# The first pair's down projection in each SwiGLU: seven products of Strassen's form, or the plain product by halves of tokens

## The chip, the cores and the metric

The kernel runs on one core of one Trainium2 chip. The metric is the device time of one launch in microseconds; below it is 2633.43 us, the median of three runs (2632.23 to 2636.09). A core has a matrix engine (TensorE, PE in the profile; its weight loads are listed apart as PEld), a vector engine (VectorE, DVE), a scalar engine (ScalarE, ACT), GpSimd (POOL) and a queue that issues the loads (SyncE, SP). Each works through its own queue in order, and they wait for one another by semaphores.

## The reference, cut to what matters

Two groups of tokens (512 and 256) go through two layers with shared weights. Each layer is a half SwiGLU, a mixer, and another half SwiGLU; so there are four SwiGLUs, all of one shape (D_MODEL 1024, D_FF 2816).

```python
def swiglu(h, wg, wu, wd):
    return (jax.nn.silu(h @ wg) * (h @ wu)) @ wd

def even_layer(x, ...):
    x = x + 0.5 * swiglu(rmsnorm(x, f1_n), f1_g, f1_u, f1_d)
    x = x + mixer_ab(rmsnorm(x, mix_n), ...)
    x = x + 0.5 * swiglu(rmsnorm(x, f2_n), f2_g, f2_u, f2_d)
    return x
...
```

The odd layer has another mixer, and a last norm follows. All of it is in float32.

## The kernel before

All 768 tokens are worked on together, features on partitions: x is eight tiles of 128 x 768. Tokens are cut into two halves of 384 (HALVES). Each float32 product is made of three faster matmuls: an operand is split into a rounded high part and the low rest, and `mm3` adds high by high, high by low and low by high into one PSUM bank. For a weight block of 128 x 512, `wsplit` does this with a cast on ScalarE (line 114, tile whi) and a subtraction on VectorE (line 115, wlo), with five tiles of each; for an activation of 128 x 384, `split` does the same (lines 196 and 197).

The 2816 hidden features are 22 blocks of 128, taken as 11 pairs. Within a pair, gate and up are computed by Strassen's method: seven products of half-size blocks in place of eight, where the blocks are halves of the inner dimension, the two feature blocks of the pair, and the two halves of tokens. Sums of weight blocks are made on VectorE (`sums`, line 609, tiles s); sums of products are made in PSUM, with copies of a bank to another (ScalarE) where a partial result is used twice. The products of a pair are called p1 to p7 and read the operands b11, b21, t1, t2, t3, n4, b22. Pairs 0 to 3 are "early": their p1 and p2 are done ahead, in the order of ORDER, so that the second half of the tokens can be normalised meanwhile. The other five follow pair by pair: p6 (t2), p7 (t3), p4 (n4), p5 (t1), p3 (b22), each with a gate and an up product of 12 matmuls. `hidden` turns the finished gate and up of one feature block i and one half of tokens into the tile h[i, half] (VectorE, ScalarE, VectorE, VectorE).

The down projection is done per two pairs, also by Strassen's method. For it, `operands(q)` prepares from the four tiles h of pair q the seven operands b11, t1, b21, t2, t3, b22, n4 (tiles d, each split into high and low; subtractions at line 432). It is a generator: the steps are taken one at a time among the products of pair q + 1, and what is left is done at its end. After pair 1, `down` runs for pair 0 alone; after pairs 3, 5, 7 and 9 it runs for the two pairs before. Pairs 9 and 10 are done plainly at the end by `down_last`, from operands made by `last_operands`. In `down`, each of the seven products splits its weight block (a sum, or a raw block), and for each of four output blocks j sums 3 matmuls for each pair into a bank. Then the bank is copied to another (line 655, ScalarE) or added into x on VectorE (line 661). The product t1 goes into four accumulators acc, which are added into x in two places at the end of the SwiGLU: in the first call this is a copy on ScalarE (line 659), later an addition on VectorE (line 661).

Weights come in raw tiles of 128 x 1024 (512 KB) by a load on SP, in a pool of four (`raw`, line 99). Each pair takes four of them (gate and up of two blocks), each down projection two for each of its pairs. PSUM has two pools of four banks, mm and aux (`psum`).

The order of TensorE's instructions is that of the program. The other engines' instructions are put in order when the kernel is built, by a list scheduler that works with priorities in program order and estimated durations; on the chip that order is fixed. `mm3` also calls `tick`, which lets chains of other work (norms, operands of the next stage) put in their next step when the planner's own clock is due.

Of the kernel before, what the change touches and what calls it, by code (L numbers as in the profile page):

```python
# [14 lines left out]
ALU = mybir.AluOpType  # L15

P = 128
D = 1024
# [5 lines left out]
H = T // 2  # L24
GROUPS = ((0, TA), (TA, T))
HALVES = ((0, H), (H, T))
# [25 lines left out]
class Trunk:  # L52
# [364 lines left out]
    def ffn(self, pre):  # L417
# [7 lines left out]
        acc = []  # L425
        d, dl = {}, {}

        def operands(q):


            h = hs.pop(q)
            sub = lambda o, x, y: nc.vector.tensor_tensor(out=o, in0=x, in1=y, op=ALU.subtract)
            d[q] = {}

            def put(n, src):
                d[q][n] = self.dtile(n), self.dtile(n)
                self.split(*d[q][n], src)

            h11, h12, h21, h22 = h[0, 0], h[0, 1], h[1, 0], h[1, 1]
            yield put("b11", h11)  # L440
            yield sub(h11, h12, h11)
            yield put("t1", h11)
            yield put("b21", h21)
            yield sub(h11, h22, h11)
            if q and q % 2 == 0:
                self.later = operands_2(h, sub, put)
                return
            for _ in operands_2(h, sub, put):
                yield

        def operands_2(h, sub, put):
            h11, h12, h21, h22 = h[0, 0], h[0, 1], h[1, 0], h[1, 1]
            yield put("t2", h11)
            yield sub(h12, h22, h12)
            yield put("t3", h12)
            yield put("b22", h22)
            yield sub(h21, h21, h11)
            yield put("n4", h21)

        def pair(p):  # L460
# [114 lines left out]
            if p:  # L575
                steps = operands(p - 1) if p < NPAIR - 1 else self.last_operands(dl, 0, hs[p - 1], acc)
# [10 lines left out]
        for p in range(NPAIR):  # L587
            for _ in stages[p]:
                pass
            if p == 1:  # L590
                acc += [self.fw.tile([P, H], F32, tag=f"p1{j}", name=f"p1{j}") for j in range(4)]
            if p % 2 and p < NPAIR - 1:
                self.down(pre, range(max(p - 2, 0), p), d, acc)
        kind = self.following[0]
        self.norm_begin(self.following)
        if kind == "f":
# [10 lines left out]
    def sums(self, a11, a12, a21, a22, s, n, name):  # L607

        f = lambda o, x, y, op: self.nc.vector.tensor_tensor(out=o, in0=x, in1=y, op=op)  # L609
        if name == "s1":  # L610
            return s[n, "s1"]
        if name == "s4":
            t = s[n, "s2"]
            f(t, a12, t, ALU.subtract)
            return t
        if name == "s2":
            t = s[n, "s1"] = self.fw.tile([P, 4, P], F32, tag="s", name="s1", bufs=8)
            f(t, a21, a22, ALU.add)
        t = s[n, name] = self.fw.tile([P, 4, P], F32, tag="s", name=name, bufs=8)
        if name == "s3":  # L620
            f(t, a11, a21, ALU.subtract)
        else:
            f(t, s[n, "s1"], a11, ALU.subtract)
        return t

    def dtile(self, name):
        return self.fw.tile([P, H], F32R, tag="e", name=f"d{name}", bufs=NE)

    def down(self, pre, pairs, d, acc):

        nc = self.nc
        a, s, bank = {}, {}, {}
        for p in pairs:
            rows = [self.raw(f"{pre}_w_down", 2 * p + k, 1, 0, D)[:, 0, :] for k in (0, 1)]
            a[p] = [t[:, i * 512 : (i + 1) * 512].rearrange("p (a b) -> p a b", a=4) for i in (0, 1) for t in rows]
        sums = lambda name: {p: self.sums(*a[p], s, p, name) for p in pairs}

        def product(w, b, key, start, out, to=None):  # L640

            st = {p: self.wsplit(w[p], nc.vector) for p in pairs}
            for j in range(4):
                new = lambda k: (self.psum(self.aux, "aux") if k in "YZ" else self.psum())[:, :H]
                if start:
                    bank[key, j] = new(key)
                ps = bank[key, j]
                for p in pairs:
                    self.mm3(
                        ps, (st[p][0][:, j, :], st[p][1][:, j, :]), d[p][b],  # L650
                        start and p == pairs[0], p == pairs[-1], not start,
                    )
                if to:
                    bank[to, j] = new(to)
                    nc.scalar.copy(bank[to, j], ps)
                if out:
                    o = acc[j] if out is acc else self.x[4 * out[0] + j][:, HALVES[out[1]][0] : HALVES[out[1]][1]]
                    if out is acc and pairs[0] == 0:
                        nc.scalar.copy(o, ps)
                    else:  # L660
                        nc.vector.tensor_tensor(out=o, in0=ps, in1=o, op=ALU.add)  # L661

        def more(n):
            for _ in range(n if len(pairs) > 1 else 0):
                next(self.later, None)

        w = {n: {p: a[p][i] for p in pairs} for i, n in enumerate(("a11", "a12", "a21", "a22"))}
        s2 = sums("s2")
        product(sums("s1"), "t1", "Z", True, acc)
        product(w["a11"], "b11", "X", True, None, "Y")  # L670
        more(3)
        product(w["a12"], "b21", "X", False, (0, 0))
        more(1)
        product(s2, "t2", "Y", False, None, "W")
        more(3)
        product(sums("s3"), "t3", "Y", False, (1, 1))
        product(sums("s4"), "b22", "W", False, (0, 1))
        product(w["a22"], "n4", "Y", False, (1, 0))
# [886 lines left out]
```

## Time and profile before

| | |
|---|---|
| Median of three runs | 2633.43 us (2632.23 to 2636.09) |
| The profiled execution | 2634.87 us |
| Its span, first to last instruction | 2633.1 us |
| Granted TensorE clock, mean | 0.99 |
| TensorE busy, instructions | 2561.3 us (97%), 15094 matmuls |
| VectorE busy | 2267.8 us (86%) |
| ScalarE busy | 1365.6 us (52%) |
| DMA | 84 GB/s over the span |

Busy time is the time in which an engine has an instruction at work; instructions of an engine overlap a little in the records, so the mean of one is somewhat longer than the distance to the next. The chain that ended last follows the execution back from its end, at each step to what released it. The four down projections of pair 0 lie at 102.42 to 116.98, 853.45 to 868.01, 1346.82 to 1361.38 and 2201.31 to 2215.87 us of the span.

### The profile page before, as it was taken

How to read it: one execution, taken by the hardware profiler on the slowest of the kernel's cores; microseconds unless marked ns; L12 is line 12 of the kernel's file. 1: busy time of each engine (PE TensorE's matmuls, PEld its weight loads, DVE VectorE, ACT ScalarE, POOL GpSimd, SP SyncE). 2: the span in 40 equal slices, each digit the busy share in tenths (PEclk: the TensorE clock that was granted, in tenths of full speed). 3: DMA queues.
4: the chain of work that ended last, by engine and by line, in shares of the span. 5: the costliest groups of instructions: out<-in, count | busy, mean ns of one | idle time of the engine just before them, and what ended most of it. 6: DMA issues, size and time to landing. Idle time of an engine off the chain costs nothing.

```text
span 2633.1 us, 41175 instructions
## 1 busy us (share of the span) xinstructions
PE 2561.3 (97%) x15094; PEld 2491.3 (95%) x15094; DVE 2267.8 (86%) x4793; ACT 1365.6 (52%) x2851; POOL 88.0 (3%) x172
## 2 busy tenths in 40 slices
PE   7999999998999999999999999999999999999997
PEld 7999999987899999999999999989998989999997
DVE  8998889889779988898999888886777699988886
ACT  7544444555655544454654544454545465454443
POOL 0000000000100000000000000001222100000000
PEclk9999999999999999999999999999999999999998
DMA  5423222421223222222322222232221332222221
GB/s 168 133 78 103 71 81 65 145 87 37 89 77 97 81 81 77 68 75 86 96 81 81 73 73 74 88 111 63 63 63 40 105 104 81 81 71 74 68 87 54
DMA packets 83898, 218.99 MB, mean 83 GB/s; under 512 B 20080, under 2 KB 32880, under 8 KB 83696
## 3 DMA queue, kind: packets, MB, share of 16 engines
q1 hardware_dynamic: 83552, 216.34, 26.5%
q8 instruction: 118, 1.93, 0.3%
q14 instruction: 84, 0.69, 0.1%
q10 hardware_dynamic: 144, 0.03, 0.0%
HBM read 206.90 MB, written 15.07 MB: 84 GB/s over the span
## 4 chain that ended last, share of the span: by engine, by line
PE 86%; DVE 9%; ACT 2%; DMA 2%; issue 1%; SPq 0%; DVEq 0%; ACTq 0%
PE ps_mm L140 54%; PE ps_aux L140 31%; DMA raw<-in_w 1%; DVE wlo L115 1%; PE ps_aux L144 1%; DVE s L609 1%; DVE xl L739 1%; ACT p L911 1%; DVE p L920 0%; DVE p L905 0%; DVE tl L197 0%; ACT whi L114 0%; ACT xh L738 0%; DVE ol L197 0%; DVE x L706 0%
## 5 line engine op out<-in xcount | busy, mean ns | idle before, releaser
L114 ACT CAST whi<-s 128x512 fp32r<-128x512 f32 x496 | 304.9, 621 | 390.6 <-DVE s L609 133.1
L114 ACT CAST whi<-raw 128x512 fp32r<-128x512 f32 x512 | 311.0, 619 | 257.8 <-PE ps_mm L140 116.8
L115 DVE TENSOR_TENSOR wlo<-s,whi 128x512 fp32r<-128x512 f32 x496 | 337.0, 685 | 61.1 <-ACT whi L114 60.8
L115 DVE TENSOR_TENSOR wlo<-raw,whi 128x512 fp32r<-128x512 f32 x494 | 337.5, 691 | 28.3 <-ACT whi L114 24.1
L140 PE MATMUL ps_aux<-dt,whi 128*128 128x384 f32 x864 | 219.3, 334 | 2.1 <-ACT whi L114 2.1
L140 PE MATMUL ps_mm<-db,whi 128*128 128x384 f32 x864 | 219.2, 334 | 0.0
L140 PEld LDWEIGHTS ps_aux<-dt,whi 128*128 128x128 f32 x864 | 156.0, 188 | 2.4 <-ACT whi L114 2.4
L140 PEld LDWEIGHTS ps_mm<-db,whi 128*128 128x128 f32 x864 | 156.1, 188 | 0.0
L140 PE MATMUL ps_mm<-xh,whi 128*128 128x512 f32 (+1 forms) x416 | 147.4, 354 | 3.8 <-ACT xh L738 3.8
L140 PE MATMUL ps_aux<-dt,wlo 128*128 128x384 f32 x432 | 144.4, 334 | 0.3 <-DVE wlo L115 0.3
L140 PE MATMUL ps_mm<-db,wlo 128*128 128x384 f32 x432 | 144.4, 334 | 0.0
L140 PE MATMUL ps_mm<-xl,whi 128*128 128x512 f32 (+1 forms) x416 | 142.3, 342 | 1.1 <-DVE xl L739 1.1
L140 PE MATMUL ps_mm<-xh,wlo 128*128 128x512 f32 (+1 forms) x416 | 142.1, 341 | 0.0
L609 DVE TENSOR_TENSOR s<-raw 128x512 f32<-128x512 f32 x124 | 85.0, 686 | 23.0 <-DMA raw<-in_w 22.9
L499 DVE TENSOR_TENSOR u<-ps_aux,u 128x384 f32<-128x384 f32 x176 | 97.0, 551 | 2.8 <-PE ps_aux L140 2.6
L609 DVE TENSOR_TENSOR s<-raw,raw 128x512 f32<-128x512 f32 x124 | 83.7, 686 | 18.2 <-DMA raw<-in_w 18.0
L140 PE MATMUL ps_aux<-dh,whi 128*128 128x384 f32 x384 | 97.6, 335 | 0.6 <-DVE x L706 0.6
L911 ACT ACTIVATE p<-p,st 128x256 f32<-128x256 f32 (+3 forms) x144 | 68.9, 480 | 55.0 <-DVE st L909 54.9
L494 ACT COPY u<-ps_mm 128x384 f32<-128x384 f32 x176 | 83.5, 474 | 24.2 <-PE ps_mm L140 24.0
L661 DVE TENSOR_TENSOR x<-ps_aux,x 128x384 f32<-128x384 f32 x160 | 86.0, 552 | 9.3 <-PE ps_aux L140 9.2
L140 PEld LDWEIGHTS ps_mm<-xh,whi 128*128 128x128 f32 x416 | 79.9, 192 | 14.1 <-ACT xh L738 4.9
L140 PE MATMUL ps_mm<-oh,whi 128*128 128x384 f32 x256 | 88.1, 344 | 4.6 <-DVE x L888 4.0
(486 smaller groups left out, 8058.2 us busy)
## 6 DMA issues: line engine op xcount, KB each, us to landing
raw<-in_w SPq DMA_DIRECT2D x350, 512.0 KB, 3.7
xdm<-x SPq DMA_DIRECT2D x16, 384.0 KB, 2.3
x<-in_x SPq DMA_DIRECT2D x16, 192.0 KB, 5.5
x<-xdm SPq DMA_DIRECT2D x8, 384.0 KB, 3.4
xold<-xdm SPq DMA_DIRECT2D x8, 384.0 KB, 3.0
out_y<-y SPq DMA_DIRECT2D x8, 384.0 KB, 2.4
tab<-skew SPq DMA_DIRECT2D x8, 256.0 KB, 4.8
raw<-in_w SPq DMA_DIRECT2D x8, 256.0 KB, 2.6
```

The costliest lines, as they stand in the source:

```text
L114: nc.scalar.copy(hi, src)
L115: (eng or nc.gpsimd).tensor_tensor(out=lo, in0=src, in1=hi.bitcast(F32), op=ALU.subtract)
L140: self.nc.tensor.matmul(out, lhsT=lhsT, rhs=rhs, start=start, stop=stop, **kw)
L144: self.nc.tensor.transpose(out, src, self.ident)
L494: nc.scalar.copy(e[n, out], bank[key, n])
L499: nc.vector.tensor_tensor(out=t, in0=bank[key, n], in1=t, op=ALU.add)
L609: f = lambda o, x, y, op: self.nc.vector.tensor_tensor(out=o, in0=x, in1=y, op=op)
L661: nc.vector.tensor_tensor(out=o, in0=ps, in1=o, op=ALU.add)
L739: nc.vector.scalar_tensor_tensor(out=lo, in0=src, scalar=gain, in1=hi.bitcast(F32), op0=ALU.mult, op1=ALU.subtract)
L911: nc.scalar.activation(outs[i], outs[i], AF.Exp, bias=nm[:, i : i + 1], accum_out=sm[:, i : i + 1])
```

## The change

In each SwiGLU, the down projection of pair 0 no longer uses Strassen's products. `operands(0)` splits the four tiles h as they are, and a new function `down_first` multiplies them by the raw weight blocks: for two halves of the output columns (i), four output blocks (j) and two halves of tokens, six matmuls go into one bank (two feature blocks, three matmuls each), and the bank is added into x. The banks of the first half of tokens are from the pool mm, those of the second from aux. Nothing of pair 0 goes into acc, so the first call of `down`, now that of pairs 1 and 2, fills acc by the copy on ScalarE. `more` always takes its steps, as `down` is no longer called for a single pair.

```diff
             def put(n, src):
-                d[q][n] = self.dtile(n), self.dtile(n)
+                name = n if isinstance(n, str) else "h"
+                d[q][n] = self.dtile(name), self.dtile(name)
                 self.split(*d[q][n], src)
 
             h11, h12, h21, h22 = h[0, 0], h[0, 1], h[1, 0], h[1, 1]
+            if q == 0:
+                for i, half in h:
+                    yield put((i, half), h[i, half])
+                return
...
             if p % 2 and p < NPAIR - 1:
-                self.down(pre, range(max(p - 2, 0), p), d, acc)
+                if p == 1:
+                    self.down_first(pre, d[0])
+                else:
+                    self.down(pre, range(p - 2, p), d, acc)
...
+    def down_first(self, pre, d):
+
+        rows = [self.raw(f"{pre}_w_down", k, 1, 0, D)[:, 0, :] for k in (0, 1)]
+        for i in (0, 1):
+            st = [self.wsplit(t[:, i * 512 : (i + 1) * 512].rearrange("p (a b) -> p a b", a=4), self.nc.vector) for t in rows]
+            for j in range(4):
+                for half, (c0, c1) in enumerate(HALVES):
+                    ps = (self.psum(self.aux, "aux") if half else self.psum())[:, :H]
+                    for k in (0, 1):
+                        self.mm3(ps, (st[k][0][:, j, :], st[k][1][:, j, :]), d[k, half], k == 0, k == 1)
+                    x = self.x[4 * i + j][:, c0:c1]
+                    self.nc.vector.tensor_tensor(out=x, in0=ps, in1=x, op=ALU.add)
...
-                    if out is acc and pairs[0] == 0:
+                    if out is acc and pairs[0] == 1:
                         nc.scalar.copy(o, ps)
...
         def more(n):
-            for _ in range(n if len(pairs) > 1 else 0):
+            for _ in range(n):
                 next(self.later, None)
```

## The prediction

> **What bounds the kernel now.** I read the page first: the shares of the engines and the chain that ended last.
>
> ```profile
> span 2633.1 us, 41175 instructions
> ...
> PE 2561.3 (97%) x15094; PEld 2491.3 (95%) x15094; DVE 2267.8 (86%) x4793; ACT 1365.6 (52%) x2851; POOL 88.0 (3%) x172
> ...
> PE 86%; DVE 9%; ACT 2%; DMA 2%; issue 1%; SPq 0%; DVEq 0%; ACTq 0%
> ```
>
> TensorE is busy for 97% of the span and is 86% of the chain; VectorE comes second, 86% busy and 9% of the chain. So a matmul that is added is paid in full unless it falls into a wait, and VectorE work that is removed is worth only the waits of TensorE that it ends. The question is how long those waits are around the four down projections of pair 0. I found these stages in the timeline by the tiles that the matmuls read and asked for the busy time in each: the stage itself, the stretch of pair 1 ahead of it, the stretch of pair 2 behind it. The first number of a row is the stretch, then come the busy times of the engines; PEclk is the granted clock.
>
> ```profile
> core 0: us, PE busy (x) PEld busy (x) DVE busy (x) ACT busy (x) POOL busy (x), PEclk, DMA share, GB/s
> 102.42:116.98 14.56, 14.56 (x85) 14.56 (x85) 14.41 (x28) 9.57 (x21) 0.00 (x0) 1.00 0.34 110
> ...
> sum 58.24, PE 58.24 PEld 58.24 DVE 56.34 ACT 38.32 POOL 0.00; mean PE 14.56 PEld 14.56 DVE 14.09 ACT 9.58 POOL 0.00
> ```
>
> Inside the stage TensorE never waits: 14.56 us in each SwiGLU, all busy, at full clock. But VectorE is full too (56.34 of 58.24 us). The stretches of pair 1 (five products, 120 matmuls) and of pair 2 (the same), summed over the four SwiGLUs:
>
> ```profile
> sum 84.04, PE 83.78 PEld 83.14 DVE 81.98 ACT 48.85 POOL 0.00; mean PE 20.94 PEld 20.79 DVE 20.50 ACT 12.21 POOL 0.00
> ...
> sum 93.70, PE 87.72 PEld 84.32 DVE 90.77 ACT 47.61 POOL 0.00; mean PE 21.93 PEld 21.08 DVE 22.69 ACT 11.90 POOL 0.00
> ```
>
> From the chain, a run of matmuls without any wait gives the price of one:
>
> ```profile
> 191.17 16.64 PE ps_mm L140 x96
> ```
>
> 16.64 / 96 = 0.1733 us, so 120 matmuls need 20.80 us and four such stretches 83.20. Pair 1 loses 84.04 - 83.20 = 0.84 us in all, pair 2 loses 93.70 - 83.20 = 10.50. Nearly all of that sits in its first step, the two t2 products of p6 (24 matmuls, 4.16 us each time):
>
> ```profile
> 116.98:123.32 6.34, 4.73 (x26) 4.10 (x26) 6.30 (x12) 2.09 (x5) 0.00 (x0) 1.00 0.34 91
> 868.01:874.32 6.31, 4.70 (x25) 4.06 (x25) 6.26 (x12) 2.07 (x5) 0.00 (x0) 1.00 0.28 80
> 1361.38:1366.74 5.36, 4.71 (x25) 4.07 (x25) 5.36 (x11) 3.57 (x7) 0.00 (x0) 1.00 0.34 96
> 2215.87:2223.67 7.80, 6.18 (x25) 5.55 (x25) 7.71 (x14) 2.55 (x5) 0.00 (x0) 0.79 0.23 68
> sum 25.81, PE 20.32 PEld 17.78 DVE 25.64 ACT 10.27 POOL 0.00; mean PE 5.08 PEld 4.45 DVE 6.41 ACT 2.57 POOL 0.00
> ```
>
> 25.81 - 16.64 = 9.17 us lost, with VectorE busy throughout (25.64). The timeline of the first SwiGLU shows why:
>
> ```profile
> 110.78 0.33 SPq L99 DMA_DIRECT2D raw<-in_w  x1
> ...
> 111.46 2.12 DVE L661 TENSOR_TENSOR x<-ps_aux,x 128x384 f32<-128x384 f32 x4
> 113.54 2.12 DVE L661 TENSOR_TENSOR x<-ps_mm,x 128x384 f32<-128x384 f32 x4
> 115.62 2.12 DVE L661 TENSOR_TENSOR x<-ps_aux,x 128x384 f32<-128x384 f32 x4
> 117.66 0.68 DVE L609 TENSOR_TENSOR s<-raw 128x512 f32<-128x512 f32 x1
> 118.25 0.69 DVE L609 TENSOR_TENSOR s<-raw,s 128x512 f32<-128x512 f32 x1
> 118.86 0.68 DVE L609 TENSOR_TENSOR s<-s,raw 128x512 f32<-128x512 f32 x1
> ...
> 120.05 1.14 ACT L114 CAST whi<-s 128x512 fp32r<-128x512 f32 x2
> ...
> 120.72 0.44 PE L140 MATMUL ps_mm<-t20h,whi 128*128 128x384 f32 x1 [1.50 <-ACT whi L114]
> ```
>
> Twelve additions into x, one behind each finished PSUM bank, occupy VectorE until 117.66. Only then come the sums of pair 2's up weights, s1 (117.66) and s2 (118.86), with another sum between; ScalarE casts at 120.05; TensorE, whose matmul for it would have followed the gate product's 12 at 116.98 + 2.08 = 119.06, goes on at 120.72. The last raw tile that these sums need was requested at 110.78, and a load lands in a median of 3.7 us:
>
> ```profile
> raw<-in_w SPq DMA_DIRECT2D x350, 512.0 KB, 3.7
> ```
>
> So the data were there at about 114.5. It is VectorE's queue, filled by the Strassen form of the down projection, that makes TensorE wait.
>
> **What the change adds.** In each SwiGLU 2 x 4 x 2 x 2 x 3 = 96 matmuls of 384 columns stand in place of 7 x 4 x 3 = 84. That is 12 more, with their weight loads beside them: 12 x 0.1733 = 2.08 us, 8.32 us in four SwiGLUs. TensorE is full in the stage, so nothing hides them. This term is nearly certain: the stage becomes 16.64 us long.
>
> **What it removes.** Durations by line, mean of one in ns after the comma:
>
> ```profile
> L115 DVE TENSOR_TENSOR wlo<-raw,whi 128x512 fp32r<-128x512 f32 x494 | 337.5, 691 | 28.3 <-ACT whi L114 24.1 <-PE ps_mm L140 0.4
> L609 DVE TENSOR_TENSOR s<-raw,s 128x512 f32<-128x512 f32 x124 | 83.0, 684 | 0.1
> L661 DVE TENSOR_TENSOR x<-ps_mm,x 128x384 f32<-128x384 f32 x160 | 86.4, 551 | 5.2 <-PE ps_mm L140 5.0
> L197 DVE TENSOR_TENSOR db<-sg,db 128x384 fp32r<-128x384 f32 x72 | 40.1, 557 | 5.1
> L432 DVE TENSOR_TENSOR u<-u,u 128x384 f32<-128x384 f32 x36 | 20.0, 556 | 0.8
> L655 ACT COPY ps_mm<-ps_aux 128x384 f32<-128x384 f32 x80 | 37.2, 465 | 26.7 <-PE ps_aux L140 23.9 <-DVE x L661 0.6 <-DVE wlo L115 0.6
> ```
>
> In pair 1 the operands of pair 0 are four splits in place of seven splits and four subtractions: 7 VectorE operations of 0.56, 3.9 us. In the down projection four weight splits in place of seven and no sums: 7 x 0.69 = 4.8 us. Together 8.7 us of VectorE per SwiGLU; operations in a row overlap by 0.08 (0.69 long, 118.25 to 118.86 apart), so about 7.6 by start times. ScalarE loses three casts and three copies of operands, and 12 copies of about 0.47 between banks and into acc; it had 9.6 us of work in 14.56 and bounds nothing. In the down projection of pairs 1 and 2, four additions into acc on VectorE become four copies on ScalarE (2.2 us moved). TensorE loses no time in the rows that I have of that later stage (the 96 matmuls at 191.17 follow it), so that is worth nothing. The loads are the same in number and size, so SP's queue keeps its order.
>
> **What stays in the stage.** Sixteen additions into x remain: 16 x 0.55 + 4 x 0.69 = 11.6 us of VectorE in 16.64 of TensorE, where it was 16.4 in 14.56 by the same means (some of it done ahead). A new group is six matmuls, 1.04 us, and its addition 0.55: VectorE has half of each group free, and there the sums of pair 2 can go, since both raw rows are free once their four splits are done. The four splits need four of the five whi tiles, two of which the last products of pair 1 return just ahead of the stage; splitting is then over about 1 us into it, the loads of the up weights land some 4 us later, and s1 and s2 with cast and split (4 x 0.69 = 2.8) are ready some 11 us before the t2 product of up at 16.64 + 2.08. Additions go alternately to two pools of four banks, and a bank comes round again after 8 x 1.04 us. What is late next is thus nothing in this stage; the product after it waits only if VectorE is still behind.
>
> **The sum.** Of the 9.17 us I take all as saved. The other waits that a VectorE backlog explains are the 0.84 in pair 1, 10.50 - 9.17 = 1.33 later in pair 2, and the first SwiGLU's pair 3:
>
> ```profile
> 144.12:149.37 5.25, 4.44 (x26) 4.12 (x25) 5.13 (x10) 3.97 (x8) 0.00 (x0) 1.00 0.30 78
> ```
>
> 5.25 - 4.16 = 1.09. Together 3.26; bounds 0 and 3.26, I take half, 1.6, because VectorE stays nearly full in pair 2, whose own work is unchanged. So 8.3 - 9.2 - 1.6 = -2.5 us. The profiled execution took 2634.87 (span 2633.1 and 1.8 around it): 2632.4. It is 1.4 above the median 2633.43, and one term fits that difference: the fourth SwiGLU lost 7.80 - 6.3 = 1.5 us more than the first two, at a low clock.
>
> ```profile
> 2219.60:2223.67 4.07, 3.94 (x12) 3.63 (x13) 4.03 (x8) 1.10 (x2) 0.00 (x0) 0.60 0.43 129
> ```
>
> If a median run has no such drop, the sum against it is 8.3 - 7.7 - 1.6 = -1.0, 2632.4 again. I forecast **2632.4 us**, from 2630.8 (all of the 3.26) to 2634.0 (none).
>
> The Trainium skill, "TensorE: Matmul & The Clock Gate", Part 1, lets the clock fall only after an idle window of about 3.4 us. Here the granted clock fell to 0.60 after 1.50 us of idle in the fourth SwiGLU, and stayed 1.00 after as much in the first two; the trace does not bear the page out as a bound. By the page the waits cost no clock, and the saving would be 7.7, the figure of the second sum.
>
> **The rivals.** *The wait stays.* VectorE's order is fixed when the kernel is built, with the 16 additions ahead of pair 2's sums in the program. If up's s1 and s2 still stand behind the last addition (0.5 us after the stage ends), cast and product come at least 1.2 + 0.6 us later, against 2.08 us of t2 product of gate to cover 0.5 + 1.8 and any sum between: TensorE stops again. The 8.3 us are then paid and the 9.2 stay; with the other 1.6 still saved it is +6.7, without them +8.3: 2640.1 to 2641.7 from the median. It decides at whether the two sums issue before the last three additions. For it: up's data were there at 114.5 before, and VectorE went on adding. Against: then its additions came one per 0.52 us, its own duration, and left no room; now one per 1.04.
>
> *All waits go, and another with them.* The first SwiGLU alone also waits in the down projection of pairs 3 and 4:
>
> ```profile
> PE ps_aux L140 <- ACT whi L114: 2.1, 1, 2.1
> ```
>
> The other three run the same code there without it, so it is an accident of order that a changed schedule may undo, 2.1 us. With all of 3.26: 8.3 - 7.7 - 3.3 - 2.1 = -4.8 from the median; with another 0.7 from the mixers, whose order may shift too (an estimate at a third of that accident), 2627.9. The same kind of accident may arise anew: two of them on top of the forecast give -1.0 + 4.2 = +3.2, 2636.6.
>
> *The bank changes slow the clock.* Groups of six matmuls change bank throughout. If these made the granted clock fall as in the row at 2219.60, where 12 matmuls took 4.07 us, 0.34 each, the 96 would last 32.6 and not 16.6 us: 4 x 16 = +64. Against: today's stage changes bank every three matmuls and has PEclk 1.00. The same page of the Trainium skill, "A second HAM failure mode: psum-queue depth-cycling", describes such a kernel; the row speaks against it here.
>
> **How the numbers follow.** Forecast 0.60, new accidents 0.08 (both within 0.2%, 5.3 us, about what a measurement of this kernel can tell from no change); the wait stays 0.20 (slower); all goes 0.10 (faster); the clock 0.02 (slower). Faster 0.10, same 0.68, slower 0.22. The range runs from 2627.9, where all goes, to 2640.5, into the lower part of the staying wait; the forecast's own is 2630.8 to 2634.0.
>
> **What would show it.** TensorE with 15142 matmuls; the stage 16.64 us, with VectorE clearly below full; the t2 step of pair 2 at 4.2 us in each SwiGLU, and additions into x with sums between them. If that step still takes over 6 us with a wait for whi, the first rival holds. If TensorE waits inside the new stage, I have misjudged splits or banks.

## The result, and the profile after

The changed kernel takes 2630.21 us (median of 22 runs, 2625.74 to 2634.12). The kernel before, run beside it, takes 2633.92 (median of 22, one of which took 8962.97 us and is left out of the ratio). The ratio is 0.9985, with an interval of 0.9979 to 0.9992. So the change is faster by 3.7 us by the medians, less than the 0.2% that I had set as the bound, which the interval just reaches. The profiled execution took 2632.34 us; its span is 2.5 us shorter than before's. First the page: span, shares of the engines, and the chain that ended last.

```profile
span 2630.6 us, 41163 instructions
...
PE 2565.3 (98%) x15142; PEld 2500.9 (95%) x15142; DVE 2235.3 (85%) x4721; ACT 1340.3 (51%) x2795; POOL 87.4 (3%) x172
...
PE 90%; DVE 7%; ACT 2%; issue 1%; DMA 0%; SPq 0%; DVEq 0%; ACTq 0%
```

TensorE has 48 matmuls more (15142 to 15094 before), VectorE 32.5 us less work. VectorE's share of the chain went from 9% to 7%. Now the same stretches as in the prediction, in busy time by windows (stretch, then PE, PEld, DVE, ACT, POOL, granted clock, DMA): the first SwiGLU's stage, the sum of the four stages, the four t2 steps of pair 2 with their sum, the sum of the four stretches of pair 1, and that of pairs 2 and 3 together.

```profile
core 0: us, PE busy (x) PEld busy (x) DVE busy (x) ACT busy (x) POOL busy (x), PEclk, DMA share, GB/s
101.53:118.17 16.64, 16.64 (x97) 16.64 (x97) 14.44 (x27) 4.01 (x8) 0.00 (x0) 1.00 0.40 121
sum 66.56, PE 66.56 PEld 66.56 DVE 57.84 ACT 15.92 POOL 0.00; mean PE 16.64 PEld 16.64 DVE 14.46 ACT 3.98 POOL 0.00
...
118.17:122.33 4.16, 4.16 (x25) 4.16 (x25) 3.01 (x5) 2.49 (x6) 0.00 (x0) 1.00 0.49 152
875.06:879.22 4.16, 4.16 (x26) 4.16 (x25) 3.95 (x7) 2.49 (x6) 0.00 (x0) 1.00 0.01 2
1365.82:1369.98 4.16, 4.16 (x26) 4.16 (x26) 3.95 (x7) 2.49 (x6) 0.00 (x0) 1.00 0.01 2
2217.69:2221.85 4.16, 4.16 (x26) 4.16 (x25) 3.95 (x7) 2.49 (x6) 0.00 (x0) 1.00 0.03 12
sum 16.64, PE 16.64 PEld 16.64 DVE 14.86 ACT 9.97 POOL 0.00; mean PE 4.16 PEld 4.16 DVE 3.71 ACT 2.49 POOL 0.00
...
sum 83.20, PE 83.20 PEld 83.20 DVE 73.29 ACT 44.66 POOL 0.00; mean PE 20.80 PEld 20.80 DVE 18.32 ACT 11.17 POOL 0.00
...
sum 166.40, PE 166.40 PEld 166.40 DVE 159.32 ACT 89.68 POOL 0.00; mean PE 41.60 PEld 41.60 DVE 39.83 ACT 22.42 POOL 0.00
```

Every one of these stretches is now as long as its matmuls: PE's busy time equals the stretch to the hundredth, and the clock is 1.00. The stage costs 66.56 us in all where it cost 58.24. The t2 steps are 4.16 us each where they were 5.36 to 7.80. Pairs 2 and 3 of before, in the same view:

```profile
sum 178.36, PE 171.57 PEld 167.36 DVE 172.92 ACT 93.05 POOL 0.00; mean PE 42.89 PEld 41.84 DVE 43.23 ACT 23.26 POOL 0.00
```

From here on I call the stage with pairs 2 and 3 behind it, up to the next down projection, "the stretch" and give it as a sum over the four SwiGLUs: 58.24 + 178.36 = 236.60 us before, 66.56 + 166.40 = 232.96 after. VectorE was busy for 229.26 of 236.60 (97%) and is for 217.16 of 232.96 (93%).

The timeline of VectorE in the first stage has the order that the prediction described: sums of pair 2's up weights (L617) between additions into x (L648).

```profile
107.97 0.56 DVE L648 TENSOR_TENSOR x<-ps_aux,x 128x384 f32<-128x384 f32 x1 [0.48 <-PE ps_aux L140]
108.44 0.68 DVE L617 TENSOR_TENSOR s<-raw 128x512 f32<-128x512 f32 x1
109.04 0.55 DVE L648 TENSOR_TENSOR x<-ps_mm,x 128x384 f32<-128x384 f32 x1
109.51 0.68 DVE L617 TENSOR_TENSOR s<-s,raw 128x512 f32<-128x512 f32 x1
110.11 0.55 DVE L648 TENSOR_TENSOR x<-ps_aux,x 128x384 f32<-128x384 f32 x1
```

One part got longer. In the first SwiGLU the time from the end of the stretch to its last down projection was 323.37 us and is 325.80, while the other three took 320.32 to 320.40 and take 320.32. Windows of before and of after for that part, and a cut of 3 us out of it:

```profile
161.85:485.22 323.37, 320.92 (x1849) 320.23 (x1849) 284.21 (x518) 155.51 (x308) 0.00 (x0) 1.00 0.28 82
```

```profile
159.77:485.57 325.80, 322.43 (x1849) 321.79 (x1849) 282.46 (x512) 156.64 (x312) 0.00 (x0) 0.99 0.27 81
...
253.00:256.00 3.00, 3.00 (x11) 3.00 (x10) 2.12 (x4) 0.00 (x0) 0.00 (x0) 0.50 0.83 252
```

The wait in the down projection of pairs 3 and 4 has grown: TensorE stands idle for 2.76 us up to 250.57 and for 0.61 us up to 251.80 (before: 2.12 and 0.33 us), and then runs 3 us at half clock, 11 matmuls where 17 would go. VectorE's timeline after the change shows what it waits for. In the first SwiGLU the two sums that this down projection needs (at 249.13 and 249.85) stand behind operations on a product that VectorE itself has to wait for; in the second they stand well ahead of the same operations (at 998.98 and 1000.06):

```profile
247.33 0.56 DVE L515 TENSOR_TENSOR v<-ps_mm,acc 128x384 f32<-128x384 f32 x1 [1.52 <-PE ps_mm L140]
...
249.13 0.69 DVE L617 TENSOR_TENSOR s<-raw,raw 128x512 f32<-128x512 f32 x1
...
998.98 0.69 DVE L617 TENSOR_TENSOR s<-raw,raw 128x512 f32<-128x512 f32 x1 [0.39 <-DMA raw<-in_w]
...
1004.93 0.55 DVE L515 TENSOR_TENSOR v<-ps_mm,acc 128x384 f32<-128x384 f32 x1
```

So this wait is one of order, in a place where VectorE has idle time. Before, one sum stood one operation earlier (250.59, behind 250.11).

So the spans differ thus: stages +8.32; pairs 2 and 3 -11.96; pair 1 -0.84 (84.04 to 83.20); the first SwiGLU's later part +2.43; the other three's -0.08; the start, the mixers and pair 0 together -0.15 (976.84 to 976.69); the end -0.26. That makes -2.5. The -0.15 hides two larger terms of opposite sign: one mixer stretch became 4.65 us longer and another 3.15 shorter, with next to nothing changed but the clock (the number before the last two of the row). Before, then after:

```profile
485.22:832.62 347.40, 332.50 (x1935) 303.09 (x1935) 292.16 (x820) 199.74 (x423) 12.03 (x9) 0.99 0.28 87
```

```profile
485.57:837.62 352.05, 336.53 (x1936) 306.57 (x1935) 292.20 (x820) 199.74 (x423) 12.02 (x9) 0.97 0.27 86
```

One profile against one other is thus good to some 4 us for the whole kernel; the stretch, all at clock 1.00 after, is good to far less. The experiments are read by their stretch first and by their ratio second.

### The profile page after: what moved, and what is told of

Same layout as the page of the kernel before. It is cut to its first block, busy times and chain, and to the rows that moved or that the text cites. A ratio compares the mean times of both kernels' runs of the same rounds, so it can differ in the third digit from the quotient of the medians.

```text
span 2630.6 us, 41163 instructions
## 1 busy us (share of the span) xinstructions
PE 2565.3 (98%) x15142; PEld 2500.9 (95%) x15142; DVE 2235.3 (85%) x4721; ACT 1340.3 (51%) x2795; POOL 87.4 (3%) x172
## 4 chain that ended last, share of the span: by engine, by line
PE 90%; DVE 7%; ACT 2%; issue 1%; DMA 0%; SPq 0%; DVEq 0%; ACTq 0%
PE ps_mm L140 56%; PE ps_aux L140 33%; DVE wlo L115 1%; PE ps_aux L144 1%; DVE xl L760 1%; ACT p L932 1%; DMA raw<-in_w 0%; DVE p L941 0%; DVE p L926 0%; DVE tl L197 0%; ACT xh L759 0%; DVE tmp L362 0%; DVE ol L197 0%; DVE x L727 0%; ACT whi L114 0%
## 5 line engine op out<-in xcount | busy, mean ns | idle before, releaser
L114 ACT CAST whi<-s 128x512 fp32r<-128x512 f32 x480 | 294.4, 621 | 422.5 <-PE ps_mm L140 132.5
L140 PE MATMUL ps_aux<-dt,whi 128*128 128x384 f32 x768 | 196.0, 336 | 2.8 <-ACT whi L114 2.8
L140 PE MATMUL ps_mm<-db,whi 128*128 128x384 f32 x768 | 194.8, 334 | 0.0
L140 PEld LDWEIGHTS ps_aux<-dt,whi 128*128 128x128 f32 x768 | 139.7, 189 | 3.1 <-ACT whi L114 3.1
L140 PEld LDWEIGHTS ps_mm<-db,whi 128*128 128x128 f32 x768 | 138.7, 188 | 0.0
L140 PE MATMUL ps_aux<-dh,whi 128*128 128x384 f32 x512 | 130.1, 335 | 0.6 <-DVE x L727 0.6
L140 PE MATMUL ps_aux<-dt,wlo 128*128 128x384 f32 x384 | 129.1, 336 | 0.6 <-DVE wlo L115 0.6
L140 PE MATMUL ps_mm<-db,wlo 128*128 128x384 f32 x384 | 128.3, 334 | 0.0
L617 DVE TENSOR_TENSOR s<-raw 128x512 f32<-128x512 f32 x120 | 82.3, 686 | 18.6 <-DMA raw<-in_w 18.5
L617 DVE TENSOR_TENSOR s<-raw,raw 128x512 f32<-128x512 f32 x120 | 80.9, 685 | 17.2 <-DMA raw<-in_w 17.2
L140 PEld LDWEIGHTS ps_aux<-dh,whi 128*128 128x128 f32 x512 | 92.3, 188 | 1.2 <-DVE x L727 0.9
L140 PE MATMUL ps_mm<-ol,whi 128*128 128x384 f32 x256 | 87.2, 341 | 2.0 <-DVE ol L197 1.7
```

The costliest lines, as they stand in the source:

```text
L114: nc.scalar.copy(hi, src)
L140: self.nc.tensor.matmul(out, lhsT=lhsT, rhs=rhs, start=start, stop=stop, **kw)
```

## The experiments

The bill is plain: 8.3 us paid, 12.8 saved. What is open is why the waits went. The prediction put it down to the place of two sums in VectorE's queue (both must issue before the last additions). The rival is VectorE's total: it was busy for 97% of the stretch, so a wait that is taken away in one place comes back in the next.

**The order alone.** Kernel before, Strassen's products kept; only the sums for the t2 products of the pair that follows are put ahead in the planner's order.

```diff
-                    with self.tc.high_priority() if early and p == EARLY - 1 else nullcontext():
+                    with self.tc.high_priority() if early and p >= EARLY - 2 else nullcontext():
```

> The kernel before, with one thing changed: the sums s1 and s2 of pair 2 (gate and up) get the high priority that pair 3's have, so that VectorE's fixed order has up's two sums among the last eight additions into x and not behind them. No operation is added or removed. 'Stretch' below is the down projection of pair 0 and the two pairs behind it, up to the next down projection; it took 236.6 us in all four SwiGLUs before, 233.0 after, and TensorE alone needs 224.6 of it in the kernel before. Theory A (VectorE's total of work in the stretch sets its length): VectorE was busy 229.3 us there, so at most 7.3 of the 12.0 us of waits can go; expected 3 to 7 us faster than before, the rest of the waits turning up later in pairs 2 and 3. Theory B (only the place of the two sums in the queue mattered): 9 to 12 us go, about 2623.

Measured: 2633.28 us, ratio 1.0000 (0.9991 to 1.0008). The edit did what it should: in the timeline the two sums stand between the last additions, and the four t2 steps behind the stage last 16.83 us, 0.19 over their matmuls. But t3 of pair 2 and t2 and t3 of pair 3 now wait, and the stretch as a whole has hardly moved. The timeline, two windows of the first SwiGLU, and the sum of the stretch:

```profile
115.30 0.68 DVE L609 TENSOR_TENSOR s<-raw 128x512 f32<-128x512 f32 x1
116.36 0.68 DVE L609 TENSOR_TENSOR s<-s,raw 128x512 f32<-128x512 f32 x1
```

```profile
116.18:120.34 4.16, 4.16 (x25) 3.98 (x25) 3.96 (x8) 2.04 (x4) 0.00 (x0) 1.00 0.00 0
...
138.09:146.03 7.94, 6.87 (x38) 6.23 (x38) 7.94 (x16) 4.56 (x10) 0.00 (x0) 1.00 0.00 0
...
sum 235.52, PE 229.22 PEld 223.82 DVE 229.43 ACT 130.85 POOL 0.00; mean PE 57.30 PEld 55.95 DVE 57.36 ACT 32.71 POOL 0.00
```

236.60 to 235.52: 1.1 us of 12.0 saved. In the window from 138.09, VectorE is busy for all of 7.94 us. The wait followed the backlog. The order of the two sums isn't what the change bought. Neither forecast came true: theory B had 9 to 12 us, and theory A had 3 to 7. VectorE's idle time in the stretch, 7.3 us before, is still 6.1, and half of that (3.0 us) is waiting for weights to land. So the stretch doesn't shrink to VectorE's busy time just because a better order is offered.

**Strassen kept, VectorE relieved through GpSimd.** Kernel before; pair 0's operand subtractions and its sums of weights go to GpSimd.

```diff
-            sub = lambda o, x, y: nc.vector.tensor_tensor(out=o, in0=x, in1=y, op=ALU.subtract)
+            sub = lambda o, x, y: (nc.vector if q else nc.gpsimd).tensor_tensor(out=o, in0=x, in1=y, op=ALU.subtract)
...
-        sums = lambda name: {p: self.sums(*a[p], s, p, name) for p in pairs}
+        sums = lambda name: {p: self.sums(*a[p], s, p, name, None if p else self.nc.gpsimd) for p in pairs}
```

> The kernel before, with the four subtractions among the operands of pair 0 and the four weight sums of its Strassen down projection done by GpSimd in place of VectorE. No matmul is added. Theory A (VectorE's total): it loses 4 x 0.47 + 4 x 0.60 = 4.3 us per SwiGLU, more than the 3.0 us of waits, so the stretch falls to TensorE's 224.6 us and the kernel is 12 us faster than before, about 2622, and 8 faster than the change. Theory B (only the order of up's sums behind the additions): the twelve additions in a row stay, 0 to 3 us. Rival to both: GpSimd is slow for such sums (a subtraction of 128x512 took 1.34 us on it in the profile of before), the products wait for it inside the stage, which then exceeds 14.56 us, and the time is not better than before.

Measured: 2651.7 us, ratio 1.0064 (1.0052 to 1.0077), slower by 17 to 19. The stretch did shorten (233.50, VectorE 221.28), but pair 1 ahead of it went from 84.04 to 100.55 us:

```profile
sum 100.55, PE 88.99 PEld 87.39 DVE 95.04 ACT 48.53 POOL 42.52; mean PE 22.25 PEld 21.85 DVE 23.76 ACT 12.13 POOL 10.63
```

The timeline shows VectorE's own instructions stretched while GpSimd works:

```profile
85.52 1.35 POOL L432 TENSOR_TENSOR u<-u,u 128x384 f32<-128x384 f32 x1
85.91 1.50 DVE L115 TENSOR_TENSOR wlo<-s,whi 128x512 fp32r<-128x512 f32 x1
92.20 1.50 POOL L609 TENSOR_TENSOR s<-s,raw 128x512 f32<-128x512 f32 x1
92.47 0.55 DVE L508 TENSOR_TENSOR sg<-ps_mm,acc 128x384 f32<-128x384 f32 x1
93.67 1.74 POOL L609 TENSOR_TENSOR s<-raw 128x512 f32<-128x512 f32 x1
94.18 1.79 DVE L609 TENSOR_TENSOR s<-raw 128x512 f32<-128x512 f32 x1
```

The split that takes 0.69 takes 1.50, the sum that takes 0.68 takes 1.79; the instruction with one operand in PSUM keeps its 0.55. So the work was not taken off VectorE in pair 1, and as a test of VectorE's total this run only half counts. Pair 1's +16.5 and the stretch's -3.1 make 13.4 of the 17.7 us by which the span grew. Most of the rest lies elsewhere: the first SwiGLU's later part takes 325.85 us (+2.5), the mixer stretch behind it 351.29 (+3.9, at a clock of 0.97), and the start is 1.7 shorter.

**VectorE's load put back.** Changed kernel; beside each of the 16 additions of the stage VectorE adds a piece of acc to itself, into a tile that nobody reads. That is 64 instructions in the four stages, of 0.55 us each.

```diff
+                    self.nc.vector.tensor_tensor(out=self.etile("more"), in0=self.acc[:, c0:c1], in1=self.acc[:, c0:c1], op=ALU.add)
```

> The changed kernel, with 16 additions of 128x384 more on VectorE in each new stage, one behind each addition into x, from and to tiles that nothing else waits for. TensorE's work is that of the change. Theory A (VectorE's total): 16 x 0.47 = 7.5 us more on VectorE per SwiGLU, 54.3 + 7.5 = 61.8 against TensorE's 58.24, so TensorE waits at least 3.6 us in each stretch: 14 to 22 us slower than the change, with waits behind the stage as before. Theory B (the Strassen form's order of sums and additions): the sums of pair 2 still fit ahead of the last additions, under 2 us.

Measured: 2634.14 us, ratio 1.0005 (0.9997 to 1.0014); beside the change's 0.9985 that is some 5 us more. The stretch:

```profile
sum 240.26, PE 236.41 PEld 232.33 DVE 238.32 ACT 105.06 POOL 0.00; mean PE 59.10 PEld 58.08 DVE 59.58 ACT 26.26 POOL 0.00
```

VectorE is full again (238.32 of 240.26), and the stretch is 7.3 us longer with no matmul added, all of it behind the stage (the four stages stay 16.64). The size is half of the least that I expected (14 us): VectorE gained only 21.2 us there, because 22 of the 64 additions ran ahead of the stage, in pair 1. VectorE's load does bring the waits back; theory B, which expected under 2 us of it, is out.

**The price of matmuls.** Changed kernel; in 12 of the 16 groups of a stage one term, low by high part of the second feature block, is left out, so the stage has 84 matmuls again.

```diff
+                        if k and (half or not i):
+                            self.mmul(ps, st[k][0][:, j, :], d[k, half][0], False, False)
+                            self.mmul(ps, st[k][0][:, j, :], d[k, half][1], False, True)
+                            self.tick()
+                        else:
+                            self.mm3(ps, (st[k][0][:, j, :], st[k][1][:, j, :]), d[k, half], k == 0, k == 1)
```

> The changed kernel, leaving out 12 of the 96 matmuls in each new stage (the low-by-high term of the second feature block, for 12 of its 16 groups), so that the stage has the 84 of before; the work of the other engines is unchanged. This is the price of the added matmuls alone: both theories expect each stage at 14.56 in place of 16.64 us and 8.3 us less than the change, about 2622. By theory A VectorE (54.3 us per stretch) is then close to TensorE's 56.2, and up to 1 us per SwiGLU may come back as waits.

Measured: 2623.94 us, ratio 0.9967 (0.9954 to 0.9979). The stages last 58.25 us together, 8.31 less, as reckoned. The stretch gained only 5.34:

```profile
sum 227.62, PE 226.01 PEld 224.39 DVE 213.83 ACT 103.87 POOL 0.00; mean PE 56.50 PEld 56.10 DVE 53.46 ACT 25.97 POOL 0.00
```

58.25 + 166.40 would be 224.65, so 2.97 us are lost again, with VectorE busy for 94% of the stretch. That isn't VectorE's work alone. In the four stretches VectorE now stands idle for 6.3 us until weights have landed, where in the change it is 0.9. In the second SwiGLU these are three waits, 2.7 us in all, the longest 1.4:

```profile
DVE s L617 <- DMA raw<-in_w: 2.7, 3, 1.4
```

So part of what the twelve matmuls cost is time in which weights land and VectorE catches up, and this run doesn't tell the two apart. It also shows that the busy share over the whole stretch is no sharp line: at 93% there was no wait in the change, at 94% there are 3 us here.

**Moving VectorE's work instead of dropping it.** Kernel before with the first experiment's edit; and the operands of pair 1 for its Strassen products are no longer made in pair 2, but in the down projection of pairs 1 and 2, beside those of pair 2.

```diff
+            if q == 1:
+                self.held = operands_2(h, sub, put)
+                return
...
-                self.later = operands_2(h, sub, put)
+                more = operands_2(h, sub, put)
+                self.later = more if q > 2 else (None for _ in zip(self.held, more))
```

> The kernel before with the early sums of the first experiment, and the second half of pair 1's operands (four splits' and two subtractions' worth, 6 VectorE operations, some 3 us) taken out of pair 2 and done in the down projection of pairs 1 and 2, where VectorE was busy 26.5 of 29.2 us. No operation is added, TensorE keeps Strassen's 84 matmuls. If VectorE's total in the stretch sets its length, the stretch falls from 235.5 (first experiment) by up to the 10.9 us that it stands above TensorE's 224.6: 6 to 11 us faster than before, 2622 to 2627, with at most 2 us of new waits per SwiGLU in the later down projection. If not, the stretch stays at 234 to 237.

Measured: 2627.64 us, ratio 0.9978 (0.9969 to 0.9987). The same kernel was run on another chip:

> The kernel of the fifth experiment again (Strassen kept, pair 1's second half of operands deferred, early sums), now on one chip with the change: expected 2 to 4 us faster than the change, about 2627 to 2628, since its stretch was 229.4 us against 233.0.

Measured: 2630.28 us, ratio 0.9984 (0.9974 to 0.9993). The stretch of the first of the two:

```profile
sum 229.43, PE 226.59 PEld 224.33 DVE 224.69 ACT 128.23 POOL 0.00; mean PE 56.65 PEld 56.08 DVE 56.17 ACT 32.06 POOL 0.00
```

Here no matmul was added and Strassen's seven products stay. VectorE has 4.6 us less to do in the stretch and the stretch is 7.2 us shorter than before's; where the work went, in the later down projection, the stage still lasts 29.12 us and VectorE is busy for 26.8 of them on the mean. This is the cleanest evidence for VectorE's load: the order alone gave 1.1, the order with 4.6 us less work 7.2. It is no proof that the total alone counts, since the step from the first experiment to this one saves 6.1 us with 4.7 less work, and moving work also changes what stands where in the queue. By the medians this run is 5.9 us faster than before, just under the 6 to 11 that I expected. The version beats the kernel before on both chips. Whether it beats the change is not settled: the change's second run stood beside it on the second chip.

> The changed kernel as it is, on the same chip as the two others of this call. Expected 3 to 4 us faster than before, about 2630; stages of 16.64 us and 41.60 behind them in each SwiGLU, as these were set by TensorE alone.

Measured: 2631.17 us, ratio 0.9988 (0.9979 to 0.9997), 0.9 us above the moved operands, where I expected 2 to 4, and with intervals that overlap. Its stretch is 233.69 (0.72 more than its matmuls need, in the third SwiGLU). Its first SwiGLU's later part is again 325.80, so that loss isn't an accident of one execution. It doesn't need the plain product either: with Strassen kept it is 325.75 with the early sums and 326.71 with the moved operands.

**How much of the relief is pair 1's.** Changed kernel; seven additions on VectorE, as many operations as the change takes out there, are put back into pair 1.

```diff
+                    for _ in range(2 if n < 3 else 1):
+                        yield nc.vector.tensor_tensor(out=etile("more"), in0=rt[:, :H], in1=rt[:, H:T], op=ALU.add)
```

> The changed kernel, with seven additions of 128x384 on VectorE put back into pair 1, one or two behind each split of pair 0's operands: as many operations as these operands lost by the change (3.3 us by start times, 0.47 each). It tells the part of the relief in pair 1 from that in the stage. If VectorE's total over pair 1, the stage and the two pairs behind it is what counts, the 3.9 us per SwiGLU that VectorE has free in the stretch take it up: 0 to 1 us of waits per SwiGLU, at most 0.84 in pair 1 as before, 0 to 4 us in all. If the relief in pair 1 was what ended the wait of the t2 products, that wait comes back with 2 us per SwiGLU, 8 us in all.

Measured: 2630.85 us, ratio 0.9993 (0.9984 to 1.0001). Pair 1 stays at 20.80 us, and the stretch is within 0.3 us of its matmuls' 232.96:

```profile
sum 233.26, PE 233.26 PEld 232.81 DVE 220.92 ACT 105.69 POOL 0.00; mean PE 58.31 PEld 58.20 DVE 55.23 ACT 26.42 POOL 0.00
```

The 28 additions ran in pair 1, where VectorE's busy time rose by 4.3 us; other work gave way to them, some of it into the stretch (VectorE +3.8 us there), and the stage took it. So the part of the relief that lies in pair 1 isn't needed; what the stage itself dropped, with its 2 us more time, is enough.

**The wait of the first SwiGLU.** In the 3 us shown of the part that grew, DMA moves 252 GB/s, so I tried to hold back tables of the next mixer that load there: alone on the changed kernel, and with the moved operands.

```diff
-        if self.spare and i >= 16:
+        if self.spare and i >= 80:
```

> The changed kernel, with the loads that build the second mixer's bias tables, one of which is queued on SP behind each weight load from the 17th on, begun at the 81st. The first SwiGLU alone loses 5.4 us in a later down projection (325.8 us from there to its last one, 320.3 in the others), and only there do these loads stand in SP's queue. If the planner puts the sums of that down projection late because of them, the 325.8 become about 320.4 and the kernel is 5 us faster than the change; if the wait has another cause, or moves to the second SwiGLU, 0.

Measured: 2632.12 us, ratio 0.9993 (0.9984 to 1.0002).

> The two edits before together, on the kernel before: the sum of what they give singly, 2617 to 2622 if both hold.

Measured: 2627.22 us, ratio 0.9978 (0.9967 to 0.9988). Neither tests the question. The loads issue at the same times with and without the edit (the first at 55.0 and 55.2 us), so their place in the program isn't what sets them, and the part lasts 325.82. The first is in effect one more run of the change (stretch 233.82), the second one more of the moved operands (229.03). Beside these two, which shared their runs of before with the first run of the moved operands, the moved operands are 4.5 to 4.9 us ahead of the change; in the other set of runs they were 0.9 ahead, with intervals that overlap, and so the comparison stays open.

**GpSimd beside the new stage.** Changed kernel with eight additions in each SwiGLU on GpSimd, both inputs in SBUF, written into the stage.

```diff
+                    if half:
+                        self.nc.gpsimd.tensor_tensor(out=self.etile("more"), in0=self.acc[:, c0:c1], in1=self.acc[:, c0:c1], op=ALU.add)
```

> The changed kernel with eight additions of 128x384 in each new stage done by GpSimd, from and to tiles that nobody else waits for; VectorE's and TensorE's work is that of the change. This measures what GpSimd does to VectorE alone, which the second experiment had mixed with late sums. If the two engines hinder each other at the SBUF, VectorE's operations that read and write only SBUF (wlo, sums) take 1.2 us or more while GpSimd works, as against 0.69, and those that read a PSUM bank (x, 0.55) keep their time; the stretch, with 3.9 us of VectorE free in each SwiGLU, grows by 0 to 3 us per SwiGLU. If GpSimd was only late, VectorE's durations stay.

Measured: 2633.07 us, a single run. The planner placed the additions ahead of the stage, in pairs 0 and 1, so the stage (16.64) and the stretch (233.60) weren't tested. The timeline there gives the price of one:

```profile
88.23 1.21 POOL L650 TENSOR_TENSOR more<-acc 128x384 f32<-128x384 f32 x1 [1.70 <-DVE dh L197]
88.67 1.31 DVE L115 TENSOR_TENSOR wlo<-s,whi 128x512 fp32r<-128x512 f32 x1
90.53 1.21 POOL L650 TENSOR_TENSOR more<-acc 128x384 f32<-128x384 f32 x1 [1.10 <-DVE dh L197]
90.97 1.18 DVE L197 TENSOR_TENSOR dh<-u,dh 128x384 fp32r<-128x384 f32 x1
```

## Why the prediction was right, and where it was off

The forecast was 2632.4, and the median is 2630.2: inside the range, 0.6 below the forecast's own lower end of 2630.8. Beside before's runs the change is 3.7 us faster, within the 0.2% that got 0.68.

*The twelve matmuls* were right: 16.64 us in each of the four stages, 8.32 in all, and the run with twelve fewer gave 8.31 back. That run adds what the step left out: 3 of those 8.3 us also spare TensorE waits, on VectorE and on the weights that it waits for, so the net price of the matmuls is about 5.3 in the stretch.

*The wait behind the stage*, 9.17 us, went entirely.

*The other waits* are the term that was mis-sized: I took half of 3.26, and all went. Pair 1 gave 0.84, pairs 2 and 3 beyond the t2 steps 11.96 - 9.17 = 2.79, together 3.63 and not 1.6. The reason given, that VectorE stays nearly full in pair 2, was a look at pair 2 alone; it comes out of the new stage with no backlog, and 217.16 of 232.96 leaves room.

*The cause* was right in naming VectorE and wrong in naming the order. I argued that the two sums wait behind twelve additions, and let the first rival be decided by whether they issue before the last three. The experiment on the order shows that they can do so and next to nothing is won: the wait moves on to later products of pairs 2 and 3. A wait with VectorE busy throughout is a debt, and the row with 25.64 of 25.81 us said so. The forecast survived because the change cuts the debt as well. I had reckoned 8.7 us per SwiGLU and 2.2 moved to ScalarE; VectorE's busy time fell by 32.5 us in all, 8.1 per SwiGLU, of which 12.1 us lie in the four stretches and 8.7 in pair 1.

*What stays in the stage* was about right: VectorE 14.44 of 16.64, sums between additions. It is less clear of full than the 11.6 I counted, as work of pair 2 moved in. The four splits come at 94.3 to 100.3 us, ahead of the stage at 101.53, earlier than the 1 us into it that I put.

*The fourth SwiGLU's low clock* is gone, PEclk 1.00 in its t2 step. *The bank changes* did no harm: groups of six matmuls, PEclk 1.00 in the first stage and PE busy for all of each.

*All waits go, and another with them*: the first half came true, the second went the other way. The wait of the first SwiGLU in the down projection of pairs 3 and 4 was to vanish (2.1 us), and the part that holds it grew by 2.43, some 1 us of it idle time and the rest low clock. That cancelled most of what I had missed in the third term: the forecast for the profile was -2.5 and -2.5 was found, but with 2.0 more saved, 2.4 lost there and some 0.5 gained in small change elsewhere. That the sum came out so well is luck. By the timeline the wait itself comes from the late place of two sums in VectorE's queue, and not from the loads that I suspected: DMA stands still in it (share 0.00 from 245 to 250 us). Why they stand late in the first SwiGLU alone stays open, and no run moved them.

## What to carry to other kernels

Where the engine that feeds TensorE is busy for 97% of a stretch, count its work over the whole stretch: putting one late instruction earlier moves the wait, and taking work away or moving it to a stage with room shortens the stretch. Where that engine has idle time, as in the wait of the first SwiGLU, the place of an instruction seems to count by the trace; no run tested it. Strassen's form saves one product in eight and pays in additions on the feeding engine; here 8.3 us of plain matmuls bought 12.8 us of waits, and moving the operands of another pair to a later stage, with two sums put earlier, ended 7.2 us of waits with the products kept. A small gain of a schedule change is read from the stretch it touches, since clock drops elsewhere moved single stretches by 3 to 5 us between two profiles.

## What the runs showed of the hardware

GpSimd isn't free help for VectorE. While GpSimd worked on two inputs in SBUF (1.2 to 1.7 us), the VectorE operations on two inputs in SBUF that are shown took 1.18 to 1.79 us where they take 0.55 to 0.69 by themselves; the one with an operand in PSUM kept 0.55. In the two runs, 58 VectorE operations with both inputs in SBUF began while one of those on GpSimd ran and ended after it: 57 of them ended 0.55 us (128x512) or 0.41 us (128x384) after it, as if each had begun near its end. An addition of 1.21 us on GpSimd made a VectorE operation some 0.6 us longer, about what VectorE would need to do it (0.55). The Trainium skill, "SBUF — State Buffer", sections "SBUF: two separate sides" and "Who interferes with whom", says that VectorE's second SBUF input and GpSimd's reads go through a shared port that one instruction holds to its end, and that a VectorE instruction with at most one SBUF input, outside the two-port modes, does not contend; these rows agree.

The granted clock falls after shorter waits than I would have thought, and not each time: 0.50 after idle times of 2.76 and 0.61 us (after, from 253), 0.60 over 4.07 us after 1.50 us (before, fourth SwiGLU), and 1.00 after as much in two other SwiGLUs and after 2.12 and 0.33 us (before, 250 to 255). Before's fourth t2 step cost 7.80 instead of 6.3 for that, so a wait can cost more than its own length.
